# A decoder layer on one core: the memory's keys computed with tokens on the partitions, and turned over DRAM

## The chip, the cores and the metric

The kernel runs on one core of a Trainium2 chip. The metric is the device time of one execution in microseconds (us). The kernel before takes 364.72 us, the median of 3 runs (364.56 to 364.76). The engines are named as in the profile: PE multiplies matrices, DVE, ACT and POOL work elementwise, SP issues most of the transfers. Each engine works through its own instructions in order and waits for the others by semaphores.

## The reference, cut to what matters

One decoder layer on 256 tokens of width 1024: a causal pooling mixer beside a self-attention, an output projection and a LayerNorm; then an attention with four heads into 256 memory tokens; then a gated feed-forward. All is float32. The change is in the keys of the memory attention:

```python
mix = jnp.concatenate([pool_out, attn_out], axis=-1) @ w_out[l]
h = layer_norm(DEEPNORM_ALPHA * h + mix, ln1_g[l], ln1_b[l])
# memory attention
q = (h @ w_xq).reshape(B_, S_, XATTN_HEADS, XATTN_HEAD_DIM)
kv = mem @ w_xkv
k = kv[..., :D].reshape(B_, M, XATTN_HEADS, XATTN_HEAD_DIM)
v = kv[..., D:].reshape(B_, M, XATTN_HEADS, XATTN_HEAD_DIM)
s = jnp.einsum('bshd,bmhd->bhsm', q, k) * (XATTN_HEAD_DIM ** -0.5)
```

`mem @ w_xkv[:, :1024]` gives 256 x 1024 keys. The scores contract over the head's width, so the keys must stand with that width on the partitions.

## The kernel before

Every product is made of three: each operand is split into a high part (`h`, a cast by ACT to float32r) and a low part (`l`, what is left, by DVE), and high x high, high x low and low x high are added in PSUM. A weight goes through three steps: SP loads it into a raw tile (`w27r`, one of 7 buffers), ACT casts it (`w27h`), DVE subtracts (`w27l`); high and low tiles have 9 buffers each. The class `Stream` orders this: `tick`, called by a projection as it goes, prepares the next weight every `pace`-th time, and not while `held` is true. A raw buffer that a split has freed is loaded at once with the weight 7 places further on (`fetch`, L111 to L124), and that load stands in SP's queue at this place of the program.

PE's order of work is the program's. The stages that matter here: values and scores of the self-attention, `u` (L730), the memory's keys `xk` (L742), in whose midst `mix_pool` (L712) puts eight matmuls; the output projection `mix` (L912) with `attend` (L682) in its midst; the memory's values `xv` (L944); the queries `xq` (L968), one head at a time, between them the scores `xscores` (L974).

The keys are made by `proj_s`: a 128 x 128 block of the weight is stationary and the memory's 256 tokens move past it, high and low side by side (512 columns), and then the weight's low part with the high tokens alone (256 columns). The result has the width on the partitions, as the scores want it. ACT and DVE add the two halves out of PSUM into a tile (L748, L749); `xk_split` makes `xkTh` and `xkTl` of it in the course of the mix.

The values are made by `proj_rows`, the other way round: 128 tokens are stationary, and a row block of the weight, 128 x 1024, moves past in pieces of 512 columns. The result has the tokens on the partitions.

Three other tiles are turned between the two forms by way of DRAM (`turned`, `landed`, L494 to L512): DVE transposes 32 x 32 blocks, one transfer writes the tile to DRAM, four read it back by quarters of 32 partitions. The self-attention's probabilities `p` do this on SP's queue (tiles `ps`, `pd`, then `pt0` and `pt1`), and so does the first LayerNorm's result (`hs`, `hd`, `hr`), which becomes `h1Th` and `h1Tl`, the operand of the queries. The memory attention's probabilities (`xs`, `xd`, `xr`) use POOL's queue.

A transfer waits until the one eight places ahead of it in its queue has landed, since they share a semaphore.

Of the kernel before, what the change touches and what calls it, by code (L numbers as in the profile page):

```python
# [8 lines left out]
F32 = mybir.dt.float32  # L9
F32R = mybir.dt.float32r  # L10
# [23 lines left out]
PR_BUFS = 6  # L34
# [5 lines left out]
def r32(t):  # L40
    return t.bitcast(F32)


class Stream:
# [121 lines left out]
    def next(self):  # L166

        i = len(self.tiles)
        return i + (2 if i < len(self.items) and self.items[i][0] == "sums" else 1)
# [28 lines left out]
    def rows(self, numbers):  # L198

        return sum(self.count(i) for i in numbers)  # L200
# [8 lines left out]
@with_exitstack  # L209
def decoder_layer(  # L210
    ctx: ExitStack, tc: tile.TileContext, x, x_t, mem_t, w_qkv, w_u, w_pool, pool_scale, w_out,
    ln1_g, ln1_b, w_xq, w_xk, w_xkv, w_xo, ln2_g, ln2_b, w_gu, w_down, ln3_g, ln3_b, out,
):
    nc = tc.nc
    cp = ctx.enter_context(tc.tile_pool(name="const", bufs=1))
    wp = ctx.enter_context(tc.tile_pool(name="weights", bufs=W_BUFS))
    ap = ctx.enter_context(tc.tile_pool(name="acts", bufs=A8_BUFS))
    sp = ctx.enter_context(tc.tile_pool(name="small", bufs=3))
# [7 lines left out]
    def a8(name, dt=F32):  # L226
        return ap.tile([P, KD, S], dt, tag="a8", name=name)
# [8 lines left out]
    ws = Stream(nc, wp)  # L236

    def cols(w, c):

        return ws.add(w[c])  # L240

    def rows(w, k0, c0, nk=1, width=D):
        return ws.add(w[k0 * P:(k0 + nk) * P, c0:c0 + width].rearrange("(k p) n -> p k n", p=P), 1)
# [15 lines left out]
    ws.cuts[0] = [slice(0, 128), slice(128, 256), slice(256, 512)]  # L259
    ws.steps = {0: (ws.cuts[0], halves), 1: (halves, [slice(0, 512)])}  # L260
    c_u = [cols(w_u, c) for c in range(2)]
    c_xk = [cols(w_xk, c) for c in range(4)]
    c_mix = [rows(w_out, k, 0) for k in range(KD)]
    c_xv = [rows(w_xkv, k, D) for k in range(KD)]
    c_xq = [cols(w_xq, c) for c in range(4)]
# [15 lines left out]
    for c in range(NFC):  # L281
        c_gu.append(ws.add(w_gu[c], 4))
        n = c - LAG
# [17 lines left out]
    def sides(name):  # L301
        return [ap.tile([P, KD // 2, 2, S], F32R, tag="a8", name=f"{name}{i}") for i in range(2)]
# [4 lines left out]
    xT, mT = sides("xT"), sides("mT")  # L307
# [33 lines left out]
    def load_norm(tag, i, v):  # L341
# [16 lines left out]
        out=tri[:, P:], in_=tri[:, P:], compare_op=OP.is_ge, fill=NEG, base=0,  # L358
# [22 lines left out]
    ALL = slice(None)  # L381
# [242 lines left out]
    def scores():  # L624
        wide = {}
        for hq in range(2):
            for j in range(2):
                wide[hq, j] = bank(f"ps{hq}{j}").rearrange("p (h s) -> p h s", h=2)
        for t in range(T):
            w = (t + 1) * P  # L630
            for hq in range(2):
                for h in range(2):
                    for j in range(2):
                        hs = slice(j * HD, (j + 1) * HD)
                        hp = 2 * hq + h
# [29 lines left out]
    def probs_out(hp):  # L665
        blocks = []
        for j in range(2):
            for t in range(T):
                pr = probs[hp // 2, t, j][:, hp % 2]
                blocks.append((3 * j + t, pr.rearrange("p (m c) -> p m c", c=P)))  # L670
        turns[hp] = turned(blocks, 6, "p")
# [24 lines left out]
    sums = {}  # L696
# [26 lines left out]
    def do_v():  # L723
        pieces = [(t, 0, 512) for t in range(T)]
        acc = {piece: accbank("pv") for piece in pieces}
        yield from proj_rows(acc, c_v, lambda k: token(xT, k), pieces, True, True, True)
        for piece in pieces:
            nc.scalar.copy(vt[:, piece[0], :], acc[piece])

    def do_u():  # L730
        for c in range(2):
            pss = [halved((accbank if c else bank)(f"pu{f}")) for f in range(2)]
            yield from proj_s(pss, c_u[c], xT)
            for f, ps in enumerate(pss):
                dst = upad[:, 2 * c + f, PADW:]
                nc.scalar.copy(dst, ps[:, 1])
                nc.vector.tensor_add(dst, ps[:, 0], dst)  # L737
                windows(2 * c + f)

    xkT = (a8("xkTh", F32R), a8("xkTl", F32R))  # L740

    def do_xk():  # L742
        for c in range(4):
            pss = [halved((accbank if c < 3 else bank)(f"pxk{f}")) for f in range(2)]
            yield from proj_s(pss, c_xk[c], mT)
            sums = xk_sums[c] = sp.tile([P, 2, S], F32, name="pr", bufs=PR_BUFS)
            for f, ps in enumerate(pss):
                nc.scalar.copy(sums[:, f], ps[:, 1])  # L748
                nc.vector.tensor_add(sums[:, f], ps[:, 0], sums[:, f])  # L749

    xk_sums = {}

    def xk_split(c):
        split(*[half[:, 2 * c:2 * c + 2, :] for half in xkT], xk_sums[c])

    v, u, xk = do_v(), do_u(), do_xk()
    ws.pace = 3
    def quads(name):
# [5 lines left out]
    pss = scores()  # L764
# [13 lines left out]
    run(u)  # L778
    ws.held = False
    ws.pace = 1  # L780
    run(xk, 6)
    ws.held = True
    run(xk, 11)
    ws.held = False
    pool_diff(0)
    pool_diff(1)
    probs_in(0)
    probs_in(1)
    run(xk, 2)
    probs_out(2)  # L790
    probs_out(3)
    run(xk, 2)
    pool_diff(2)
    run(xk, 2)
    pool_diff(3)
    ws.pace = 3
    run(xk, 9)
    probs_in(2)
    probs_in(3)
    ws.pace = 2  # L800
    run(xk, 6)
    ws.held = True
    run(xk, 12)
    mix_pool()
    ws.held = False
    run(xk, 5)
    ws.held = True
    run(xk)
    ws.held = False
# [7 lines left out]
    class Norm:  # L817
# [11 lines left out]
        def sum(self, c0, c1, acc):  # L829
            s = slice(c0, c1)  # L830
            nc.vector.scalar_tensor_tensor(self.r[:, s], self.tok[:, s], ALPHA, acc, op0=OP.mult, op1=OP.add)
# [74 lines left out]
    def h1_split(t):  # L906
        raw = turns1[t].rearrange("p i k b -> p k i b")
        for k0 in (0, 4):
            h, l = [h[:, k0:k0 + 4, t * P:(t + 1) * P].rearrange("p k (i b) -> p k i b", i=4) for h in h1T]
            split(h, l, raw[:, k0:k0 + 4])  # L910

    mix = project(c_mix, lambda k: (cT[0][:, k], cT[1][:, k]), 4)  # L912
    run(mix, 2)
    xk_split(0)
    xk_split(1)
    ws.held = True
    run(mix, 2)
    load_norm("g", 1, ln1_g)()
# [1 line left out]
    run(mix, 1)  # L920
    attend()
    ws.held = False
    run(mix, 2)
    xk_split(2)
    xk_split(3)
    norms = [Norm(1, xt[:, t, :], h1[:, t, :]) for t in range(T)]
    for half in HALVES:
        norms[0].add(*half, until(mix)[1])
# [9 lines left out]
    run(mix)  # L938
    ws.held = False
    h1T = (a8("h1Th", F32R), a8("h1Tl", F32R))  # L940

    xv = [ap.tile([P, T, D], F32R, tag="a8", name=f"xv{i}") for i in range(2)]

    def do_xv():  # L944
        acc = {piece: (bank if piece == PIECES[2] else accbank)("xv") for piece in PIECES}
# [4 lines left out]
    def xv_split(t):  # L950

        for _, c0, c1 in PIECES[2 * t:2 * t + 2]:
            split(xv[0][:, t, c0:c1], xv[1][:, t, c0:c1], xvs[t, c0, c1])

    xvs = {}
    gv = do_xv()
    run(gv, 6)
    h1_split(0)
    run(gv, 4)
    h1_split(1)  # L960
    run(gv)
    xv_split(0)


# [203 lines left out]
    acc = {}  # L1168
# [8 lines left out]
    for c in range(1, NFC):  # L1177
        sgs.append(sp.tile([P, 2, T, P], F32, name="sg", tag="pr", bufs=PR_BUFS))
        pss = {t: second[t] if c == 1 else accbank("pg") for t in range(T)}
# [185 lines left out]
    for c0, c1, left in quarters:  # L1365
# [2 lines left out]
        store(1, norm.r, c0, c1)  # L1368


_INS = ["x", "x_t", "mem_t", "w_qkv", "w_u", "w_pool", "pool_scale", "w_out", "ln1_g", "ln1_b", "w_xq", "w_xk",
        "w_xkv", "w_xo", "ln2_g", "ln2_b", "w_gu", "w_down", "ln3_g", "ln3_b"]


# [41 lines left out]
```

## Time and profile before

| | |
|---|---|
| median of 3 runs | 364.72 us |
| the profiled execution's own time | 364.02 us |
| its span, first to last instruction | 362.2 us |
| PE busy | 356.8 us, 98% |
| DVE busy | 313.1 us, 86% |
| ACT busy | 201.9 us, 56% |
| POOL busy | 61.0 us, 17% |
| moved by DMA | 89.22 MB, 246 GB/s on average |

The profile is of one execution. 1.8 us of its time lie outside the span. A matmul's end is modelled and overlaps the next one's start, so the pace of a stage is read from where its first matmul and the next stage's first matmul stand in the chain of waits, not from the durations.

### The profile page before, as it was taken

The numbers are of one execution on the slowest core, as the hardware profiler recorded it, in microseconds if no ns is written. First come the engines' busy times: TensorE is split into PE (matmuls) and PEld (weight loads), VectorE is DVE, ScalarE is ACT, GpSimd is POOL, SyncE is SP. The second block draws the span as 40 slices with busy tenths as digits, with TensorE's granted clock in tenths as the row PEclk, the third lists the DMA queues.
The fourth block names the chain that finished last, engine by engine and source line by source line (L and its number), as shares of the span: only waits on it lengthen the run. The fifth ranks groups of instructions, "written<-read, shape, count | busy, mean of one in ns | idle before, by whom it ended". The sixth has DMA issues, their size and how long they took to land.

```text
span 362.2 us, 5435 instructions
## 1 busy us (share of the span) xinstructions
PE 356.8 (98%) x1843; PEld 304.4 (84%) x1843; DVE 313.1 (86%) x477; ACT 201.9 (56%) x317; POOL 61.0 (17%) x82
## 2 busy tenths in 40 slices
PE   8999999999999999999999999999999999999995
PEld 7887888888888899988888888888888888888884
DVE  5878999985999888775879989999998999879984
ACT  5857776375362765465037636744754754679301
POOL 1000009400000003320110024225303413400000
PEclk9999999999999999999999999999999999999999
DMA  7997388799936996943107887888879779658211
GB/s 247 419 419 281 116 286 314 227 329 316 371 148 208 375 373 219 340 137 135 58 0 239 320 283 243 292 293 302 297 253 346 246 256 313 218 172 260 85 58 58
DMA packets 35771, 89.22 MB, mean 246 GB/s; under 512 B 4256, under 2 KB 14368, under 8 KB 35616
## 3 DMA queue, kind: packets, MB, share of 16 engines
q1 hardware_dynamic: 34544, 86.92, 68.5%
q0 software_dynamic: 624, 1.57, 1.3%
q10 hardware_dynamic: 576, 0.39, 0.3%
q8 instruction: 14, 0.23, 0.2%
q14 instruction: 13, 0.11, 0.1%
HBM read 81.53 MB, written 7.34 MB: 245 GB/s over the span
## 4 chain that ended last, share of the span: by engine, by line
PE 98%; DMA 1%; ACT 0%; ACTq 0%; issue 0%
PE pg L376 11%; PE pg L375 11%; PE pg L374 11%; PE pxq L392 6%; PE pqk L548 6%; PE acc L374 6%; PE acc L376 6%; PE acc L375 6%; PE pxk L418 4%; PE x L376 2%; PE x L375 2%; PE x L374 2%; PE pxk L414 2%; PE pu L418 2%; PE xv L376 2%; PE xv L375 2%
## 5 line engine op out<-in xcount | busy, mean ns | idle before, releaser
L1098 POOL TENSOR_TENSOR sraw<-gr 128x128 f32<-128x128 f32 x9 | 8.7, 962 | 94.8 <-DMA gr<-gd 69.7
L847 POOL TENSOR_TENSOR rs<-mv,mhalf 128x1 f32<-128x1 f32 x6 | 4.4, 731 | 104.3 <-DVE mv L845 104.3
L703 POOL TENSOR_TENSOR win<-upad 128x271 f32<-128x271 f32 x4 | 3.5, 882 | 52.5 <-DVE upad L737 52.5
L478 ACT CAST h2Th<-tp 128x512 fp32r<-128x512 f32 x4 | 2.4, 588 | 14.5 <-PE tp L489 14.5
L1099 POOL TENSOR_TENSOR sraw<-sraw,gr 128x128 f32<-128x128 f32 x9 | 10.2, 1134 | 0.7
L1078 ACT ACTIVATE sg<-pg 128x256 f32<-128x256 f32 x22 | 7.8, 379 | 2.8 <-PE pg L376 2.7
L479 DVE TENSOR_TENSOR gTl<-gr,gTh 128x512 fp32r<-128x512 f32 x11 | 8.6, 780 | 0.7 <-ACT gTh L478 0.7
L478 ACT CAST gTh<-gr 128x512 fp32r<-128x512 f32 x11 | 6.8, 614 | 3.7 <-DMA gr<-gd 3.7
L1100 POOL TENSOR_TENSOR sraw<-gr 128x128 f32<-128x128 f32 x9 | 8.5, 945 | 0.0
L1079 DVE TENSOR_TENSOR sg<-sg,pg 128x256 f32<-128x256 f32 x22 | 8.3, 413 | 0.1
L510 POOL DMA_DIRECT2D xr<-xd x12 | 6.6, 554 | 8.7 <-DMA xd<-xs 6.3
L607 ACT ACTIVATE pr<-pr,mx 128x256 f32<-128x256 f32 (+1 forms) x12 | 5.5, 460 | 4.5 <-DVE mx L653 4.5
L607 ACT ACTIVATE xpr<-xs,mx 128x256 f32<-128x256 f32 x8 | 3.7, 470 | 7.6 <-DVE mx L618 7.6
L499 DVE STREAM_TRANSPOSE gs<-sg 128x512 f32<-128x512 f32 x11 | 7.7, 701 | 0.1
L478 ACT CAST S<-sraw 128x384 fp32r<-128x384 f32 (+1 forms) x9 | 4.7, 523 | 5.0 <-POOL sraw L1100 5.0
L502 POOL DMA_DIRECT2D xd<-xs x3 | 1.9, 629 | 33.4 <-DVE xs L499 33.4
L1336 ACT ACTIVATE minus<-ident 128x128 f32<-128x128 f32 x1 | 0.3, 311 | 12.8 <-DVE r L858 12.8
L852 DVE SCALAR_TENSOR_TENSOR r<-r,mv,g 128x512 f32<-128x512 f32 (+1 forms) x10 | 7.0, 727 | 0.2
L838 DVE BATCH_NORM_STATS2 st<-r 128x6 f32<-128x512 f32 (+1 forms) x10 | 6.4, 637 | 0.3
L1103 POOL TENSOR_TENSOR S<-gr,sraw 128x128 f32<-128x128 f32 x8 | 6.6, 828 | 0.0
L748 ACT COPY pr<-pxk 128x256 f32<-128x256 f32 x8 | 2.6, 376 | 7.2 <-PE pxk L414 7.2
L981 PE MATMUL xs<-xkTh,xq 128*128 128x256 f32 x32 | 6.4, 283 | 0.0
(1363 smaller groups left out, 1409.2 us busy)
## 6 DMA issues: line engine op xcount, KB each, us to landing
gd<-gs SPq DMA_DIRECT2D x11, 256.0 KB, 5.6
gr<-gd SPq DMA_DIRECT2D x44, 64.0 KB, 2.0
pd<-ps SPq DMA_DIRECT2D x4, 384.0 KB, 4.1
pt<-pd SPq DMA_DIRECT2D x16, 96.0 KB, 5.7
g<-in_ln_g SPq DMA_DIRECT2D x3, 512.0 KB, 5.4
b<-in_ln_b SPq DMA_DIRECT2D x3, 512.0 KB, 7.2
wr<-in_w_qkv SPq DMA_DIRECT2D x5, 256.0 KB, 4.6
mr<-in_mem_t SPq DMA_DIRECT2D x1, 1024.0 KB, 11.8
```

The source lines that it names most:

```text
L374: nc.tensor.matmul(ps, wa, ya, start=start, stop=False, skip_group_check=part)
L375: nc.tensor.matmul(ps, wa, yb, start=False, stop=False, skip_group_check=part)
L376: nc.tensor.matmul(ps, wb, ya, start=False, stop=stop, skip_group_check=part)
L392: nc.tensor.matmul(pss[f], w[:, s], y, start=k == 0 and f == 0 and n == 0, stop=k == KD - 1 and n == 2, skip_group_check=True)
L418: nc.tensor.matmul(pss[f], hi[:, s], both, start=k == 0, stop=False, skip_group_check=True)
L478: nc.scalar.copy(h, ps)
L479: nc.vector.tensor_sub(l, ps, r32(h))
L548: nc.tensor.matmul(qk[i][f][:, n], w[:, c * P:(c + 1) * P], both[:, n], start=k == 0 and n.start == 0 and (n.stop == 2 or part in first), ...
L607: nc.scalar.activation(dst[:, j, :], src[:, j, :], AF.Exp, bias=mx[:, j:j + 1], scale=sign, accum_out=sm[:, j:j + 1])
L1098: nc.gpsimd.tensor_add(s1, a21, a22)
L1099: nc.gpsimd.tensor_sub(s2, s1, a11)
L1100: nc.gpsimd.tensor_sub(s3, a11, a21)
```

## The change

The keys are made like the values: `do_xk` keeps 128 memory tokens stationary and moves row blocks of `w_xkv[:, :1024]` past them, into four banks of PSUM that it holds to its end, two of them (`accbank`) among the four that the mix accumulates in. Then DVE transposes the four banks into two tiles `ms`, and POOL writes them to DRAM (`md`, 512 KB each). After `attend` POOL reads them back in eight transfers into a tile of their own, `xkr`. `xk_split` comes near the end of the values, two splits of 128 x 1024. The copy of the weight by columns, `w_xk`, is gone. The calls of `run(xk, n)` are scaled, as a step is now three matmuls of 512 columns.

```diff
-    c_xk = [cols(w_xk, c) for c in range(4)]
+    c_xk = [rows(w_xkv, k, 0) for k in range(KD)]
...
     def do_xk():
-        for c in range(4):
-            pss = [halved((accbank if c < 3 else bank)(f"pxk{f}")) for f in range(2)]
-            yield from proj_s(pss, c_xk[c], mT)
-            sums = xk_sums[c] = sp.tile([P, 2, S], F32, name="pr", bufs=PR_BUFS)
-            for f, ps in enumerate(pss):
-                nc.scalar.copy(sums[:, f], ps[:, 1])
-                nc.vector.tensor_add(sums[:, f], ps[:, 0], sums[:, f])
...
-    def xk_split(c):
-        split(*[half[:, 2 * c:2 * c + 2, :] for half in xkT], xk_sums[c])
+        pieces = [(t, c0, c0 + 512) for t in range(T) for c0 in (0, 512)]
+        acc = {piece: (bank if piece[0] else accbank)("pxk") for piece in pieces}
+        for k in range(KD):
+            for t, c0, c1 in pieces:
+                hi, lo = ws.get(c_xk[k], 0)
+                three(acc[t, c0, c1], pair(token(mT, k), ALL, slice(t * P, (t + 1) * P)),
+                      (hi[:, c0:c1], lo[:, c0:c1]), k == 0, k == KD - 1)
+                if t and c0:
+                    ws.done(c_xk[k], 0)
+                yield
+        for t in range(T):
+            turnk[t] = turned([(4 * n, acc[piece].rearrange("p (m c) -> p m c", c=P))
+                               for n, piece in enumerate(pieces[2 * t:2 * t + 2])], KD, "m", nc.gpsimd)
+
+    def xk_in(t):
+        if not t:
+            xk_rows[0] = ap.tile([P, T, 4, KD, 32], F32, tag="a8", name="xkr")
+        turnk[t] = landed(turnk[t], KD, "m", nc.gpsimd, raw=xk_rows[0][:, t])
+
+    def xk_split(t):
+        split(*[x[:, :, t * P:(t + 1) * P].rearrange("p m (i b) -> p m i b", i=4) for x in xkT],
+              turnk[t].rearrange("p i m b -> p m i b"))
...
     run(mix, 2)
-    xk_split(0)
-    xk_split(1)
...
     attend()
     ws.held = False
+    for t in range(T):
+        xk_in(t)
     run(mix, 2)
-    xk_split(2)
-    xk_split(3)
...
     h1_split(1)
+    xkT = (a8("xkTh", F32R), a8("xkTl", F32R))
+    run(gv, 2)
+    xk_split(0)
+    run(gv, 2)
+    xk_split(1)
     run(gv)
```

SP's queue in the last third of `xk`, where the second half of the probabilities (`pt1`, printed as `pt`) is read back for `attend`. `w35r` to `w37r` are loads of raw weights:

```order
 L123 DMA w34r<-in_w_out 128x1024
 L123 DMA w35r<-in_w_xkv 128x1024
-L510 DMA pt_861<-pd 32x4x192 x8
 L123 DMA w36r<-in_w_xkv 128x1024
+L510 DMA pt_844<-pd 32x4x192 x8
 L123 DMA w37r<-in_w_xkv 128x1024
```

The load of `w36` now stands ahead of the eight reads instead of behind them, and the eighth read now waits for `w36r` to land, where it waited for `w35r`.

DVE's order from the last split of the LayerNorm's result (`h1Tl`) to the split of the first head's queries (`xq`), in the values and the first queries:

```order
 L479 TENSOR_TENSOR h1Tl<-hr,h1Th 128x4x128 x2
 L149 TENSOR_TENSOR w48l<-w48r,w48h 128x1024
+L479 TENSOR_TENSOR xkTl<-xkr,xkTh 128x8x128
 L149 TENSOR_TENSOR w49l<-w49r,w49h 128x1024
+L479 TENSOR_TENSOR xkTl<-xkr,xkTh 128x8x128
 L149 TENSOR_TENSOR w50l<-w50r,w50h 128x1024
-L479 TENSOR_TENSOR xv_1223<-xv,xv_1222 128x512 x2
+L479 TENSOR_TENSOR xv_1356<-xv,xv_1355 128x512 x2
 L149 TENSOR_TENSOR w51l<-w51r,w51h 128x1024
 L149 TENSOR_TENSOR w52l<-w52r,w52h 128x1024
-L483 SCALAR_TENSOR_TENSOR xq_1466<-pxq,xq_1465 128x512
+L483 SCALAR_TENSOR_TENSOR xq_1425<-pxq,xq_1424 128x512
```

The two splits of the keys, 1024 elements wide each, now stand between the LayerNorm's result and the queries' split.

DVE's order at the end of `xk` and in the mix:

```order
 L149 TENSOR_TENSOR w31l<-w31r,w31h 128x1024
-L749 TENSOR_TENSOR pr<-pxk_920,pr 128x256
-L749 TENSOR_TENSOR pr<-pxk_921,pr 128x256
+L499 STREAM_TRANSPOSE ms<-pxk 128x4x4x32 x4
 L149 TENSOR_TENSOR w32l<-w32r,w32h 128x1024
 L149 TENSOR_TENSOR w33l<-w33r,w33h 128x1024
-L479 TENSOR_TENSOR xkTl<-pr,xkTh 128x512 x2
```

Four transposes of 128 x 512 out of PSUM take the place of two additions, and two splits of 128 x 512 are gone; two more are gone behind `w35l`.

## Rows read from the trace of the kernel before

**Rows 1.** The page, part 4: the chain that ended last, shares by engine

```profile
PE 98%; DMA 1%; ACT 0%; ACTq 0%; issue 0%
```

**Rows 2.** Chain of waits, 52 to 77 us: start, us, engine, tile, line, count

```profile
52.61 3.65 PE pxk L418 x16
56.26 1.91 PE pxk L414 x16
...
70.00 1.73 PE pm L716 x8
...
76.61 0.23 PE acc L374
```

**Rows 3.** Chain of waits, 100 to 132 us

```profile
101.43 0.23 PE xv L374
...
123.19 7.55 PE pxq L392 x63
130.74 1.32 PE xs L981 x11
```

**Rows 4.** The tile pxk: nanoseconds min/median/max, first and last start

```profile
L748 ACT COPY pr<-pxk x8: 372/377/380, 58.1 to 76.8; 128x256 f32<-128x256 f32 x8
L749 DVE TENSOR_TENSOR pr<-pxk,pr x8: 406/410/418, 59.7 to 78.3; 128x256 f32<-128x256 f32 x8
```

**Rows 5.** The page, part 5: busy us, mean ns | idle before, releaser

```profile
L499 DVE STREAM_TRANSPOSE gs<-sg 128x512 f32<-128x512 f32 x11 | 7.7, 701 | 0.1
...
L502 POOL DMA_DIRECT2D xd<-xs x3 | 1.9, 629 | 33.4 <-DVE xs L499 33.4
```

**Rows 6.** Timeline of DVE: start, us, instruction, [idle before it <- releaser]

```profile
75.64 1.23 DVE L149 TENSOR_TENSOR w30l<-w30r,w30h 128x1024 fp32r<-128x1024 f32 x1 [0.46 <-ACT w30h L147]
...
90.13 1.28 DVE L479 TENSOR_TENSOR xkTl<-pr,xkTh 128x512 fp32r<-128x512 f32 x2
...
121.34 1.29 DVE L479 TENSOR_TENSOR h1Tl<-hr,h1Th 128x512 fp32r<-128x512 f32 x2
...
124.47 1.23 DVE L149 TENSOR_TENSOR w49l<-w49r,w49h 128x1024 fp32r<-128x1024 f32 x1 [0.70 <-ACT w49h L147]
...
130.28 0.68 DVE L483 SCALAR_TENSOR_TENSOR xq<-pxq,xq 128x512 fp32r<-128x512 f32 x1
```

**Rows 7.** Timeline of SP's queue

```profile
72.61 0.46 SPq L123 DMA_DIRECT2D w35r<-in_w_xkv  x1
74.62 5.90 SPq L510 DMA_DIRECT2D pt<-pd  x8
80.62 0.38 SPq L123 DMA_DIRECT2D w36r<-in_w_xkv  x1
...
114.46 0.38 SPq L123 DMA_DIRECT2D w47r<-in_w_xq  x1
```

**Rows 8.** DMA issues, 45 to 130 us: KB each, median us to landing

```profile
hd<-hs SPq DMA_DIRECT2D x2, 512.0 KB, 2.6
...
w35r<-in_w_xkv SPq DMA_DIRECT2D x1, 512.0 KB, 7.6
...
w47r<-in_w_xq SPq DMA_DIRECT2D x1, 512.0 KB, 4.6
```

**Rows 9.** The tile pt: all its transfers, then only the one issued last

```profile
DMA to landing us min/median/max: 2.0/5.7/8.4
...
DMA to landing us min/median/max: 3.5/3.5/3.5
```

**Rows 10.** Timeline of PE in attend

```profile
85.37 0.65 PE L690 MATMUL po<-pt,vt 128*64 128x256 f32 x4
```

**Rows 11.** Stretches: us, busy PE, PEld, DVE, ACT, POOL, PEclk, DMA share, GB/s

```profile
80.00:82.00 2.00, 2.00 (x11) 1.65 (x10) 2.00 (x3) 0.12 (x1) 0.00 (x0) 1.00 0.69 170
...
92.00:94.00 2.00, 2.00 (x10) 1.67 (x9) 2.00 (x3) 1.61 (x2) 0.00 (x0) 1.00 1.02 418
...
102.00:104.00 2.00, 2.00 (x11) 1.65 (x10) 2.00 (x3) 1.38 (x2) 0.00 (x0) 1.00 0.00 0
```

More of the change, by code (lines that the diff above doesn't have):

```diff
@@ L211, in decoder_layer @@
     ctx: ExitStack, tc: tile.TileContext, x, x_t, mem_t, w_qkv, w_u, w_pool, pool_scale, w_out,
-    ln1_g, ln1_b, w_xq, w_xk, w_xkv, w_xo, ln2_g, ln2_b, w_gu, w_down, ln3_g, ln3_b, out,
+    ln1_g, ln1_b, w_xq, w_xkv, w_xo, ln2_g, ln2_b, w_gu, w_down, ln3_g, ln3_b, out,
 ):
@@ L738, in do_u @@
                 windows(2 * c + f)
-    xkT = (a8("xkTh", F32R), a8("xkTl", F32R))
+    turnk = {}
     def do_xk():
-        for c in range(4):
-            pss = [halved((accbank if c < 3 else bank)(f"pxk{f}")) for f in range(2)]
-            yield from proj_s(pss, c_xk[c], mT)
-            sums = xk_sums[c] = sp.tile([P, 2, S], F32, name="pr", bufs=PR_BUFS)
-            for f, ps in enumerate(pss):
-                nc.scalar.copy(sums[:, f], ps[:, 1])
-                nc.vector.tensor_add(sums[:, f], ps[:, 0], sums[:, f])
-    xk_sums = {}
-    def xk_split(c):
-        split(*[half[:, 2 * c:2 * c + 2, :] for half in xkT], xk_sums[c])
+        pieces = [(t, c0, c0 + 512) for t in range(T) for c0 in (0, 512)]
[11 more added lines that the diff above has]
+                               for n, piece in enumerate(pieces[2 * t:2 * t + 2])], KD, "m", nc.gpsimd)
+    xk_rows = {}
+    def xk_in(t):
[5 more added lines that the diff above has]
+              turnk[t].rearrange("p i m b -> p m i b"))
     v, u, xk = do_v(), do_u(), do_xk()
@@ L780, in decoder_layer @@
     ws.pace = 1
-    run(xk, 6)
+    run(xk, 3)
     ws.held = True
-    run(xk, 11)
+    run(xk, 5)
     ws.held = False
@@ L788, in decoder_layer @@
     probs_in(1)
-    run(xk, 2)
+    run(xk, 1)
     probs_out(2)
     probs_out(3)
-    run(xk, 2)
+    run(xk, 1)
     pool_diff(2)
-    run(xk, 2)
+    run(xk, 1)
     pool_diff(3)
     ws.pace = 3
-    run(xk, 9)
+    run(xk, 5)
     probs_in(2)
@@ L800, in decoder_layer @@
     ws.pace = 2
+    run(xk, 3)
+    ws.held = True
     run(xk, 6)
-    ws.held = True
-    run(xk, 12)
     mix_pool()
     ws.held = False
-    run(xk, 5)
+    run(xk, 2)
     ws.held = True
@@ L940, in decoder_layer @@
     h1T = (a8("h1Th", F32R), a8("h1Tl", F32R))
-    xv = [ap.tile([P, T, D], F32R, tag="a8", name=f"xv{i}") for i in range(2)]
     def do_xv():
@@ L960, in decoder_layer @@
     h1_split(1)
+    xkT = (a8("xkTh", F32R), a8("xkTl", F32R))
[3 more added lines that the diff above has]
+    xk_split(1)
     run(gv)
+    xv = [ap.tile([P, T, D], F32R, tag="a8", name=f"xv{i}") for i in range(2)]
     xv_split(0)
@@ L1368, in decoder_layer @@
         store(1, norm.r, c0, c1)
-_INS = ["x", "x_t", "mem_t", "w_qkv", "w_u", "w_pool", "pool_scale", "w_out", "ln1_g", "ln1_b", "w_xq", "w_xk",
-        "w_xkv", "w_xo", "ln2_g", "ln2_b", "w_gu", "w_down", "ln3_g", "ln3_b"]
+_INS = ["x", "x_t", "mem_t", "w_qkv", "w_u", "w_pool", "pool_scale", "w_out", "ln1_g", "ln1_b", "w_xq", "w_xkv", "w_xo", "ln2_g", "ln2_b", "w_gu", "w_down", "ln3_g", "ln3_b"]
 def kernel(**inputs):
@@ L1403 @@
     given["w_qkv"] = np.concatenate([first.ravel(), w_in[3 * P:, 512:1536].ravel(), blocks(w_in[:, 1536:], pairs)])
-    given["w_u"], given["w_xk"] = chunks(given["w_in"][:, :512]), chunks(given["w_xkv"][:, :D])
+    given["w_u"] = chunks(given["w_in"][:, :512])
     given["w_xq"] = chunks(given["w_xq"])
```

## The prediction

> **What bounds the kernel now.** I read the chain that ended last first. Its shares by engine [rows 1] leave 98% to PE: the kernel is as long as PE's work, and a saving on another engine is worth nothing by itself. Then the same chain in order of time around the change. The keys begin at 52.61 and the mix at 76.61, with 1.73 of `pm` (the pooling mixer's matmuls) inside [rows 2]; the values run from 101.43 to 123.19, then the queries and the first scores [rows 3]. No wait stands between them. So the gain is what PE saves in the keys, and each rival is a wait that PE doesn't have today. For those I read the timelines of SP and DVE up to the instruction that would release PE, and last the DMA share by stretch, since the change adds traffic.
>
> **The keys on PE.** Before they cost 76.61 - 52.61 - 1.73 = 22.27 us: four chunks of 16 matmuls of 512 columns and 16 of 256, 3.65 and 1.91 a chunk [rows 2], which is 228 and 119 ns each. Removed are 128 matmuls, added 96 of 512 columns. The columns stay 49,152. What is added needs no estimate: the values are the same loop over the same stationary tokens with a weight of the same size, 8 row blocks x 4 pieces x 3 = 96 matmuls, in 123.19 - 101.43 = 21.76 us, 227 ns each [rows 3]. The gain is 22.27 - 21.76 = 0.51, and this is all that the change can give on PE.
>
> The Trainium skill ("TensorE: Matmul & The Clock Gate", section Back-to-back issue gap) gives N/2.4 + 2.5 ns for an isolated gap at the full clock, 216 and 109 ns. By it the keys would go from 64 x 325 ns = 20.8 us to 96 x 216 ns = 20.7 us, an estimate of 0.1 saved. The rows are above it, and by more at 256 columns, so the 0.51 of the rows stands.
>
> **DVE and ACT around the keys.** ACT loses eight copies of 377 ns, DVE eight additions of 410 ns [rows 4] and four splits of 0.64 (a row of two takes 1.28 [rows 6]). DVE gains four transposes, 0.70 each from SBUF [rows 5]; no row shows one from PSUM, so between 0.7 and twice that, taken at 0.75. All of it lies beside PE. It could reach PE in one place: the mix's third and fourth bank are the keys' first two, and PE wants them 6 and 9 matmuls after its start, 1.36 and 2.04 us. In DVE's order one weight split stands before the transposes. The one that stands in its place now began at 75.64, after waiting for ACT, and took 1.23 [rows 6]; PE and the pooling mixer come about 0.4 earlier, so the two transposes run from about 76.5 to 78.0, and PE, at the mix from 76.1, wants the banks at 77.5 and 78.1. Cost nothing, cover 0.1 to 0.3; from PSUM at twice the price it costs up to 1.4.
>
> **The reads for `attend`.** In SP's queue `w36r` moves ahead of the eight reads of `pt1`. The last read now goes out when `w36r` has landed. Before, it went out when `w35r` had, 72.61 + 7.6 = 80.2 [rows 7, 8], and landed 3.5 later, at 83.7 [rows 9]. A load of 524 KB at the 418 GB/s of a full stretch [rows 11] takes 1.25, so the last read goes out at 81.45 and lands at 84.95. PE wants it at the last group of `attend`, 85.37 before [rows 10] and 84.86 now: a wait of 0.1. With the quickest landing, 2.0 [rows 9], it is early by 1.4. The hop adds to it: DVE's transposes end near 78.0 and 79.5, and POOL then writes twice 524 KB, 1.25 each, against the same reads. DMA is idle for 0.62 in 80 to 82 [rows 11]. Of the first write 0.63 doesn't fit there, and about half of this lies ahead of the last read: 0.3. If both writes go ahead, the wait is 0.1 + 2.5 = 2.6. I take 0.4, with ends at 0 and 2.6, near the low one because the measured landing gives 0.1.
>
> **The key splits at the end of the values.** DVE has from the end of the LayerNorm's split, 121.34 + 1.29 = 122.63, to the queries' split, 130.28 to 130.96 [rows 6]. PE wants that at the ninth matmul of the first scores: 130.74 + 8 x 0.12 = 131.70 [rows 3]. Two splits are put between, 1.14 each by the spacing of weight splits, and take up the 0.70 that DVE waited there [rows 6]: 1.58 later, at 132.54, counted from the same start. PE comes at 131.70 - 0.51 + 0.4 = 131.59. Alone it would cost 0.95. The cover is an earlier start: DVE loses 1.28 at 90.13 [rows 6], and what follows there, the first LayerNorm and its hop, is a row of DVE work that moves up by that much; so does the load of `w47`, which goes out behind the hop at 114.46 and lands 4.6 later [rows 7, 8], just ahead of the split in question. With 1.2 earlier and the 0.4 of `attend` later, DVE is done at 131.7, the same 0.1 as PE. I take 0; the ends are 0 and, if the start is half a us later than today, 1.4.
>
> The 10 transfers that POOL issues, about 0.6 each [rows 5], cost nothing: POOL has no other work until the LayerNorm.
>
> **The sum.** -0.51 + 0.4 + 0 = -0.1. On the profiled execution's own 364.02 (its span, 362.2, and 1.8 around it) that is 363.9; the median is 0.7 above that execution, so I carry the difference to it: 364.72 - 0.1 = 364.6.
>
> **Rivals.** *All waits are hidden.* Then the 0.51 stays: 364.2. For it: the last read can land 1.4 early, and the hop's writes may use what is idle. Against it: three covers of 0.1 to 0.3 would have to hold at once.
>
> *The hop's traffic makes the key splits late.* Place: DVE between the LayerNorm's split and the queries' split. The hop moves 2.1 MB, 5.0 us at 418 GB/s, in a stretch where DMA is full but for 0.62 in 80 to 82 and all of 102 to 104 [rows 11]; some 2 us are left over, just where the LayerNorm's hop (2.6 to land [rows 8]) and `w47` are to come early. Then the start is not 1.2 earlier but up to 0.5 later, and PE waits 0.95 to 1.4 at the first scores beside the 0.4 in `attend`: -0.51 + 0.4 + 1.3 = +1.2, 365.9. It decides from the point where `w47r` goes out later than about 113.5. Against it: it takes all 5.0 us as additive, though SP's small reads leave a third of 80 to 82 unused. The Trainium skill ("DMA: Bandwidth & Descriptors", section Issuing engines are not separate DMA queues) says that transfers started by SP and by POOL run on the same 16 engines and interleave, and that a second issuing engine saves only the time to issue; by that rule the hop takes its full 5.0 from SP's loads, and this rival would be the forecast.
>
> *The transposes or the reads hold PE in the mix.* By the ends above 1.4 or 2.6 in place of 0 and 0.4: 366.0 to 366.8. For it: the cover at the banks is 0.1 to 0.3. Against it: both ends take the worst of each row.
>
> **How the numbers follow.** About 0.2%, 0.73 us, is what a measurement of this kernel can tell from no change. The forecast has a chance of 0.36, all waits hidden 0.28, the late key splits 0.28, the hold in the mix 0.08. The forecast's own range is 364.2 to 365.2. Faster than 363.99 needs more than the 0.51 that PE can save: 0.05, out of the second case. Slower than 365.45 hold the last two cases but for 0.03, and a little of the forecast's upper end: 0.35. The rest, 0.60, is within. The range goes from 364.0, under the hidden case, to 366.1, which leaves about 0.1 above.
>
> **What would show it.** In the changed profile 96 matmuls of `pxk` should take 21.7 to 21.8 without `pm`; another pace makes the first term wrong. In `attend` a wait of PE for `pt` of 0.1 to 1.0 should stand before the last groups; none means the hidden case. At the first scores a wait of PE for DVE's `xq` of 0.9 or more, with `w47r` issued after 113.5, shows the late splits. A wait of `acc` for DVE's transposes at the mix's third bank shows the last rival. The forecast is wrong if PE saves 0.5 and the time moves by more than 0.7 either way.

## The result, and the profile after

The changed kernel takes 368.13 us, the median of 4 runs (367.33 to 368.46), beside 364.73 us for the kernel before in the same runs (364.56 to 364.76). The ratio is 1.0091, 95% interval 1.0074 to 1.0109: slower by 3.4 us, outside the range of 364.0 to 366.1. The profiled execution took 368.03, with a span of 366.3 where the kernel before had 362.2. In the table of the experiments the medians are of all runs, while the ratios leave out four runs that took over 1.5% more than the fastest of their kernel (two of writes only, one each of late reads and held loads).

The page, part 4, shares by engine of the chain that ended last, answers to [rows 1]:

```profile
PE 64%; DVE 13%; DMA 13%; issue 4%; ACT 3%; SPq 2%; POOL 1%; DVEq 0%; ACTq 0%; POOLq 0%
```

PE is still 98% busy, but 26% of the chain now runs over DVE and DMA, and 36% over everything but PE: work ahead of PE has become what sets the end. What PE waited for (us in total, times, longest):

```profile
PE xs L995 <- DVE xq L483: 1.2, 1, 1.2
...
PE pxq L392 <- DVE h1Tl L479: 0.6, 1, 0.6
PE xo L375 <- DVE xst L479: 0.3, 1, 0.3
PE xs L995 <- ACT xq L482: 0.3, 1, 0.3
```

None of the four was there before. `xs` are the scores of the memory attention; `xo` multiplies its probabilities with the values, and `xst` is the split of these probabilities behind their own hop. PE's timeline, where the stages begin (answers to [rows 2, 3, 10]):

```profile
53.03 0.40 PE L374 MATMUL pxk<-w19h,mT 128*128 128x512 f32 x1
...
76.55 0.39 PE L374 MATMUL acc<-w27h,cTh 128*128 128x512 f32 x1
...
85.59 0.65 PE L690 MATMUL po<-pt,vt 128*64 128x256 f32 x4
...
124.14 0.39 PE L392 MATMUL pxq<-h1Tl,w43h 128*128 128x256 f32 x1 [0.62 <-DVE h1Tl L479]
...
132.08 0.39 PE L995 MATMUL xs<-xkTh,xq 128*128 128x256 f32 x1 [0.25 <-ACT xq L482]
...
134.49 0.74 PE L995 MATMUL xs<-xkTh,xq 128*128 128x256 f32 x4 [1.19 <-DVE xq L483]
```

Counted against the same matmul of the kernel before, PE is 0.6 late when the keys begin (the first stage, whose program is the same in both, went slower in this execution; in the second profile of the kernel before it is 0.4 late too), 0.1 late at the mix, 0.2 at the values, 1.0 after the wait for `h1Tl`, 3.0 after the two waits for the queries' split, 3.8 after the wait for `xst`, and 4.1 at the end. Each wait costs 0.2 to 0.5 more than its idle time.

SP's queue, answers to [rows 7]:

```profile
72.30 0.39 SPq L123 DMA_DIRECT2D w36r<-in_w_xkv  x1
73.86 6.34 SPq L510 DMA_DIRECT2D pt<-pd  x8
...
102.86 0.33 SPq L502 DMA_DIRECT2D hd<-hs  x1
108.20 1.75 SPq L510 DMA_DIRECT2D hr<-hd  x4
110.05 0.38 SPq L502 DMA_DIRECT2D hd<-hs  x1
113.48 2.93 SPq L510 DMA_DIRECT2D hr<-hd  x4
116.51 0.38 SPq L123 DMA_DIRECT2D w47r<-in_w_xq  x1
```

The LayerNorm's first write (`hd`) goes out 0.76 earlier than before and takes 5.3 to land in place of 2.6; its second stands behind the late reads and takes 3.4; `w47r` goes out 2.05 later. The stretches show why (the columns of [rows 11]: PEclk, DMA share and GB/s at the end):

```profile
80.00:82.00 2.00, 2.00 (x11) 1.63 (x10) 1.88 (x2) 0.00 (x0) 0.49 (x1) 1.00 1.09 340
92.00:94.00 2.00, 2.00 (x10) 1.66 (x9) 2.00 (x3) 0.78 (x1) 0.00 (x0) 1.00 1.03 289
102.00:104.00 2.00, 2.00 (x11) 1.65 (x10) 1.97 (x4) 1.74 (x2) 0.00 (x0) 1.00 1.03 420
```

The idle time of 80 to 82 and of 102 to 104 is gone, and in 92 to 94 full engines move 289 GB/s in place of 418, while the hop is read back. The kernel before had more idle time there than [rows 11] show. Its stretches from 80 to 106, the same columns:

```profile
80.00:90.00 10.00, 10.00 (x65) 8.05 (x64) 5.67 (x7) 4.42 (x8) 0.00 (x0) 1.00 0.91 287
90.00:98.00 8.00, 8.00 (x37) 6.63 (x36) 7.93 (x11) 3.61 (x4) 0.00 (x0) 1.00 1.07 404
98.00:102.00 4.00, 4.00 (x20) 3.30 (x19) 3.90 (x8) 2.53 (x3) 0.56 (x1) 1.00 0.74 260
102.00:106.00 4.00, 4.00 (x19) 3.33 (x18) 3.86 (x8) 2.43 (x3) 0.00 (x0) 1.00 0.32 131
```

By these shares 4.1 of the 26 us were idle; in the changed kernel the same four stretches have 1.02 to 1.04. DVE's timeline, answers to [rows 5, 6]:

```profile
77.13 2.50 DVE L499 STREAM_TRANSPOSE ms<-pxk 128x512 f32<-128x512 f32 x4
...
94.89 0.68 DVE L843 SCALAR_TENSOR_TENSOR r<-xt,acc 128x512 f32<-128x512 f32 x1
...
122.26 1.22 DVE L149 TENSOR_TENSOR w47l<-w47r,w47h 128x1024 fp32r<-128x1024 f32 x1 [3.90 <-ACT w47h L147]
123.40 1.28 DVE L479 TENSOR_TENSOR h1Tl<-hr,h1Th 128x512 fp32r<-128x512 f32 x2
...
128.01 1.22 DVE L479 TENSOR_TENSOR xkTl<-xkr,xkTh 128x1024 fp32r<-128x1024 f32 x1
...
133.75 0.68 DVE L483 SCALAR_TENSOR_TENSOR xq<-pxq,xq 128x512 fp32r<-128x512 f32 x1
```

DVE reaches the LayerNorm 1.0 earlier (94.89 against 95.88 before). It loses 0.2 of this to the load of the LayerNorm's bias `b`, a third transfer that lands late: 16.2 us after its issue, 9.7 in the kernel before. The chain of waits has it:

```profile
83.32 16.22 DMA b<-in_ln_b
```

Then DVE stands idle for 3.9 us until `w47` is there. `h1Tl` is 2.06 late, the queries' split 3.47.

### The profile page after: what moved, and what is told of

Its sections match the earlier page's. It is cut to its first block, busy times and chain, and to the rows that moved or that the text cites. A ratio compares the mean times of both kernels' runs of the same rounds, so it can differ in the third digit from the quotient of the medians.

```text
span 366.3 us, 5373 instructions
## 1 busy us (share of the span) xinstructions
PE 358.9 (98%) x1811; PEld 304.1 (83%) x1811; DVE 313.3 (86%) x471; ACT 199.4 (54%) x307; POOL 68.7 (19%) x92
## 4 chain that ended last, share of the span: by engine, by line
PE 64%; DVE 13%; DMA 13%; issue 4%; ACT 3%; SPq 2%; POOL 1%; DVEq 0%; ACTq 0%; POOLq 0%
PE pg L375 11%; PE pg L374 11%; PE pg L376 11%; DMA b<-in_ln_b 4%; PE pqk L548 4%; PE acc L374 3%; PE acc L375 3%; PE acc L376 3%; PE pxq L392 3%; PE x L375 2%; PE x L374 2%; DMA w49r<-in_w_xq 2%; PE x L376 2%; DMA xr<-xd 2%; DMA wr<-in_w_qkv 2%
## 5 line engine op out<-in xcount | busy, mean ns | idle before, releaser
L1112 POOL TENSOR_TENSOR sraw<-gr 128x128 f32<-128x128 f32 x9 | 9.5, 1060 | 92.9 <-DMA gr<-gd 50.3
L1114 POOL TENSOR_TENSOR sraw<-gr 128x128 f32<-128x128 f32 x9 | 9.5, 1055 | 0.0
L995 PEld LDWEIGHTS xs<-xkTh,xq 128*128 128x128 f32 x32 | 5.2, 191 | 1.9 <-DVE xq L483 1.4
L703 POOL TENSOR_TENSOR win<-win 128x269 f32<-128x269 f32 (+2 forms) x6 | 6.7, 1109 | 0.5
```

Source lines behind the costliest of these rows:

```text
L703: nc.gpsimd.tensor_add(nxt[:, 2 * n - 1:], cur[:, 2 * n - 1:], cur[:, n - 1:PADW + S - n])
L995: nc.tensor.matmul(ps[:, t, :], w, xkT[n][:, 2 * h + kk], start=not (low or t or kk or n), stop=bool(low and kk), skip_group_check=True)
L1112: nc.gpsimd.tensor_add(s1, a21, a22)
L1114: nc.gpsimd.tensor_sub(s3, a11, a21)
```

## The experiments

Theory A: the hop adds DMA work where the engines are full, the LayerNorm's hop and `w47` land late, and PE waits for whichever transfer is then last. Rival B: the two splits in DVE's order are the loss. Theory C and rival D came with the second series. C: the reads of `pt` stand on an edge, and the hop's writes push them over it in some executions. D: the traffic costs the same wherever it is put. Each series shares its runs of the kernel before. The changed kernel itself differs by 1.7 us between its two series, for a reason that no run shows, so versions of different series can't be told apart more finely than that. "Profiled" is the time of the one execution that left the profile, often one of the slower; "waits" are PE's largest behind the first stage in that profile, in us (`r` is the LayerNorm's first addition, `po` the products of `attend`, `tp` a transpose on PE); "w31" is the landing time of the load of `w31` in that profile, which goes out near 60, ahead of everything the change adds.

| kernel | median, range (runs) | before | ratio, 95% interval | profiled | waits | w31 |
|---|---|---|---|---|---|---|
| changed | 368.13, 367.33 to 368.46 (4) | 364.73 | 1.0091, 1.0074 to 1.0109 | 368.03 | `h1Tl` 0.6, `xq` 1.5 | 7.3 |
| changed again | 369.80, 369.22 to 371.50 (5) | 364.73 | 1.0149, 1.0129 to 1.0170 | 369.33 | `pt` 2.5 | 9.2 |
| no hop | 365.20, 364.05 to 366.13 (12) | 364.52 | 1.0019, 1.0009 to 1.0028 | 365.90 | `xst` 1.1 | 8.0 |
| early splits | 368.26, 366.58 to 371.05 (6) | 364.52 | 1.0095, 1.0078 to 1.0112 | 371.05 | `pt` 3.9 | 10.1 |
| no hop, early splits | 364.67, 363.94 to 365.76 (11) | 364.52 | 1.0004, 0.9994 to 1.0014 | 364.67 | `xst` 0.3 | 7.2 |
| traffic alone | 367.79, 367.36 to 368.91 (5) | 364.52 | 1.0097, 1.0083 to 1.0112 | 367.52 | `h1Tl` 1.0 | 8.5 |
| writes only | 367.80, 365.01 to 372.85 (8) | 364.73 | 1.0062, 1.0031 to 1.0092 | 369.42 | `pt` 2.2 | 9.7 |
| pt first, early splits | 368.32, 367.08 to 371.39 (6) | 364.73 | 1.0119, 1.0085 to 1.0153 | 371.39 | `r` 2.1, `pt` 0.9 | 9.7 |
| late reads | 369.37, 367.27 to 373.21 (6) | 364.73 | 1.0127, 1.0094 to 1.0160 | 373.21 | `pt` 3.2, `h1T` 1.4 | 9.3 |
| spread | 369.86, 367.89 to 371.85 (6) | 364.57 | 1.0147, 1.0123 to 1.0172 | 369.80 | `h1T` 3.1 | 7.9 |
| late writes | 373.63, 370.20 to 373.96 (6) | 364.57 | 1.0231, 1.0204 to 1.0258 | 373.43 | `h1T` 5.1, `r` 0.9 | 9.6 |
| held loads | 369.00, 366.30 to 372.10 (7) | 364.57 | 1.0096, 1.0064 to 1.0128 | 369.06 | `pt` 2.5, `h1Tl` 1.0 | 9.7 |
| turn on PE | 370.64, 369.19 to 371.08 (4) | 364.57 | 1.0159, 1.0143 to 1.0174 | 370.60 | `tp` 3.5 | 8.8 |
| turn in the gap | 366.35, 366.25 to 367.33 (5) | 364.43 | 1.0055, 1.0043 to 1.0067 | 366.30 | `po` 0.8 | 9.5 |
| half traffic | 367.34, 366.87 to 368.40 (5) | 364.43 | 1.0084, 1.0070 to 1.0098 | 367.34 | `r` 1.3, `h1Tl` 0.6 | 7.2 |
| order alone | 364.48, 364.14 to 366.11 (12) | 364.43 | 1.0007, 0.9996 to 1.0018 | 364.14 | none | 9.2 |
| before again | 364.46, 364.24 to 366.97 (11) | 364.43 | 1.0006, 0.9994 to 1.0019 | 364.46 | none | 8.1 |

### Traffic or splits: two by two, and the traffic by itself

**No hop.** 

> The changed kernel without the hop: DVE's four transposes go straight into the tile xkr, nothing is written to DRAM and nothing read back (so the keys' blocks are not exchanged between the quarters of partitions; this exchange is what is left out, 2.1 MB of traffic). The two splits stay where the change put them. Theory A (the hop's traffic keeps the DMA engines full to 106, so the LayerNorm's hop and the load of w47 come 2.06 late, and the two splits add 1.58 to that): w47r goes out at 113.2 to 114.0 in place of 116.51, no wait of PE at the first queries, 0 to 0.3 at the first scores, 364.2 to 365.0 us; 0.6 more if the first stage is as late as in the changed kernel's profile. Rival B (it is the two splits in DVE's order alone): the wait at the first scores stays at 1.0 or more, 367.0 to 368.0 us.

```diff
-            turnk[t] = turned([...], KD, "m", nc.gpsimd)
+            xk_in(t)                     # only takes the tile xkr
+            for n, piece in enumerate(pieces[2 * t:2 * t + 2]):
+                nc.vector.transpose(turnk[t][...], acc[piece]...)
```

**Early splits.** 

> The changed kernel with its hop, but the two key splits stand ahead of the LayerNorm's splits, after the second and fourth step of the values. Theory A: the traffic is the same, so w47r still goes out near 116.5 and PE still waits 0.6 at the first queries; the queries' split comes 2 earlier and the wait of 1.2 at the first scores goes: 366.2 to 366.8 us. Rival B: all of the loss goes, 364.2 to 364.8 us.

```diff
 gv = do_xv()
+    run(gv, 2); xk_split(0); run(gv, 2); xk_split(1); run(gv, 2)
-    run(gv, 6)
     h1_split(0)
...
-    run(gv, 2); xk_split(0); run(gv, 2); xk_split(1)
```

**Both.** 

> Both edits at once: no hop (the exchange of blocks between quarters of partitions is left out) and the key splits ahead of the LayerNorm's. Theory A: no wait of PE is left and the 0.51 us that the keys save on PE stays: 364.0 to 364.6 us, the same as no hop alone within 0.4. Rival B: the same as early splits alone. If a loss of 0.6 in the first stage belongs to the changed program and not to one execution, all of these stand 0.6 higher.

**Traffic alone**, in the kernel before. 

> The kernel before with the traffic alone: after the keys POOL writes 1 MB to DRAM (four writes of 256 KB out of the last tile of the keys) and after attend reads 1 MB back by eight transfers into a tile that nobody uses. Nothing else is changed. Theory A: the LayerNorm's hop lands 2 us later, w47r goes out near 116.5, PE waits 0.6 to 1.0 at the first queries and not at the first scores, 365.3 to 365.9 us. Rival B: the traffic costs nothing, 364.6 to 364.9 us.

```diff
+        for t in range(T):               # at the end of do_xk
+            turnk[t] = hp.tile([P, 4, KD * 32], F32, name="md")
+            for n in range(2):
+                nc.gpsimd.dma_start(turnk[t][:, 2 * n:2 * n + 2], xk_sums[3])
...
     attend()
     ws.held = False
+    for t in range(T):
+        xk_in(t)
```

Without the hop 365.20: 2.7 of the 3.4 us are gone, with the splits where the change put them (A's range ends at 365.0, or 365.6 with a late first stage; the wait of 1.1 for `xst` was not in it). SP's queue then runs as it should:

```profile
102.38 0.33 SPq L502 DMA_DIRECT2D hd<-hs  x1
104.97 1.75 SPq L510 DMA_DIRECT2D hr<-hd  x4
...
113.22 0.38 SPq L123 DMA_DIRECT2D w47r<-in_w_xq  x1
```

`hd` lands in 2.6 and `w47r` goes out at 113.22, the 1.2 earlier that the prediction's cover asked for. The splits are worth 0.5 (365.20 to 364.67), with intervals that overlap. With the hop, moving them gains nothing (368.26), so B falls; A's 366.2 to 366.8 was missed as well. The traffic alone costs the kernel before 3.3 us, nearly the loss of the change, with neither rows nor splits; A named the place (`w47r` at 117.13, a wait of 1.0 for `h1Tl`) but priced it at a third: PE is 1.7 late at the first queries and 3.4 behind `xo`, where it waits again, as it also does without the hop. The early splits brought what no theory had: a wait of 3.9 for `pt`, in the slowest of the six executions.

The hop's DMA work is read from the page, part 3 (queue, kind, packets, MB, share of 16 engines). POOL's queue before, and after:

```profile
q0 software_dynamic: 624, 1.57, 1.3%
```

```profile
q0 software_dynamic: 1296, 3.67, 3.0%
```

3.0% of 366.3 less 1.3% of 362.2 is 6.3 us for 2.1 MB; the prediction had 5.0. This counts POOL's packets alone, not what SP's loads lose beside them.

### Where the wait stands, and what decides it

**Changed again.** 

> The changed kernel once more, nothing edited, for its spread and a second profile. In the kernel with early splits PE waited 3.9 us for the reads of pt in attend, and then ran 6 us at half the clock; in the first profile of the changed kernel it did not wait there at all, though both have the same program up to that place. Theory C (the reads of pt stand on an edge, and the hop's writes push them over it in some executions): PE waits for pt again here, or the times spread by 2 us or more. Theory A: the wait is 0 to 0.3, and the loss is again at the first queries and scores; 367.3 to 368.5 us by both.

In this execution PE waited for nothing at the queries. It lost its time in `attend`. The chain of waits, 74 to 92 us:

```profile
74.51 9.07 DMA w36r<-in_w_xkv
83.58 0.02 issue
83.60 4.77 DMA pt<-pd
88.37 0.14 issue
88.51 0.66 PE po L690 x4
```

The last read of `pt` goes out when `w36r` has landed, 9.07 after its issue, and takes 4.77 beside the hop's writes: the mechanism of "Reads for attend", at its far end. PE idled 2.51, and then the clock fell (stretches, columns as above):

```profile
86.00:90.00 4.00, 1.49 (x11) 1.20 (x12) 0.69 (x1) 0.58 (x2) 2.83 (x6) 0.99 1.01 362
90.00:94.00 4.00, 4.00 (x13) 3.11 (x12) 3.71 (x4) 4.00 (x6) 1.57 (x3) 0.58 1.02 318
94.00:98.00 4.00, 4.00 (x19) 3.34 (x18) 3.88 (x4) 1.80 (x2) 0.00 (x0) 1.00 1.03 284
```

After the idle time the granted clock is 0.58 in 90 to 94, mostly the lower of its two levels: 13 matmuls where the full clock does 19. PE is 3.1 late at the last `po` and 4.7 to 5.0 at the first scores. C holds as a second place of the same loss: this series has a wait for `pt`, and a median 1.7 above the first, which lies outside the 367.3 to 368.5 of both theories.

**Writes only.** 

> The changed kernel with the hop's two writes of 512 KB but without the eight reads: DVE's transposes go into xkr, POOL writes xkr to DRAM, and the splits take xkr as it is (the exchange of blocks between the quarters of partitions is left out). Theory A: half of the traffic, in a stretch that had 0.62 us of idle DMA; DMA is done by 103.5 in place of 106, the LayerNorm's first write lands in 2.6 to 4 in place of 5.3, 365.2 to 366.4 us. Theory C: the writes alone are what pushes the reads of pt, PE waits there in some executions, 366 to 368 us.

```diff
     # as without the hop, and behind the two transposes:
+            via = hp.tile([P, 4, KD * 32], F32, name="md")
+            nc.gpsimd.dma_start(via, turnk[t].rearrange("p j m b -> p j (m b)"))
```

PE waits 2.2 for `pt`, as C has it; the times run from 365.01, the level without the hop, to 372.85. Its q0 has 2.0% of 367.6, so the writes are 2.6 us of DMA work and the reads the other 3.6.

**Order alone**, in the kernel before. 

> The kernel before with one edit: the second half of the probabilities is read back three steps later, so that the load of w36 goes out ahead of the reads of pt in SP's queue, as in the change. No hop, the keys by columns. Theory A: the reads of pt have cover enough without the hop's writes: 364.4 to 365.2 us, no wait for pt. If the order in SP's queue alone makes pt late: 366 us or more, with a wait for pt of 1 us or more.

```diff
-    probs_in(2); probs_in(3)
     ws.pace = 2
-    run(xk, 6)
+    run(xk, 3); probs_in(2); probs_in(3); run(xk, 3)
```

**Before again.** 

> The kernel before once more, for a second profile. The first reads of pt took 8.53 us to go out in its first profile and 7.2 to 10 in the changed versions, ahead of any traffic of the hop. If that is a spread of the landings that every kernel has, its second profile may show 7 to 10 too, and its time stays 364.2 to 365.2 us, since the cover ahead of attend takes it up.

The order alone costs nothing measurable, in a profile whose `w31` took 9.2 to land; three of its twelve executions took 365.6 to 366.1, and one of the eleven of "before again" 366.97. So the table sorts by two things. The second, the landing of `w31`, was only observed, in one profile of each kernel; no run set it. With the hop's full writes out before `attend`, all six profiles whose `w31` landed in 9.2 to 10.1 wait for `pt`, and the two at 7.3 and 8.5 do not. Without those writes, four at 8.8 to 9.6 do not (in one of them, the turn in the gap, PE also comes 2.2 later). The landing isn't fixed in the kernel before either (8.6 and 8.1 in its two profiles, 9.2 in the order alone, the same program up to there); the cover ahead of `attend` takes this up, until the writes use that cover.

### Can the debt be placed where it costs nothing?

**Reads of pt first, early splits.** 

> The changed kernel with the key splits ahead of the LayerNorm's, and with the reads of pt back in front of the load of w36 in SP's queue, as the kernel before has them. Theory C: without the wait for pt only the wait of 0.6 at the first queries is left: 366.0 to 366.8 us, 1.5 or more below early splits alone. Theory A alone (no part of the loss in attend): the same as early splits alone, 367.8 to 368.6 us.

```diff
     ws.pace = 3
-    run(xk, 5)
-    probs_in(2); probs_in(3)
+    run(xk, 3)
+    probs_in(2); probs_in(3)
+    run(xk, 2)
```

The wait for `pt` is 0.9, but DVE now waits 2.0 for `w39`, the LayerNorm's first addition is late, and PE waits 2.1 for its bank (`r`). The gain that C promised is not there; 368.32 lies in the range that A alone gave.

**Late reads.** 

> A version meant to be best: the changed kernel with the reads of pt in front of w36, the hop's eight reads issued after the second half of the LayerNorm (about 106.6 in place of 84.65, where the kernel before leaves the DMA engines half idle), one key split behind the LayerNorm's first split and one behind its second. Theory A: the LayerNorm's first write lands in 2.6 again, w47r goes out at 113.5 to 115, PE waits 0 to 0.6 in all: 364.2 to 365.4 us. Rival D (the traffic costs the same wherever it is put, since the engines only owe it to a later load): 367 us or more.

```diff
     norms[1].finish()
+    for t in range(T):
+        xk_in(t)
     h1_in(0)
```

The hop's reads, issued at 110.19, meet the LayerNorm's second write, which takes 5.6 to land; `w47r` goes out at 121.49, in the slowest of the six executions, where PE waits 3.2 for `pt` too. D's time is right here.

**Spread, late writes, held loads.** 

> The changed kernel with four moves: the reads of pt back in front of w36, the hop's two writes issued by ACT behind attend (about 87 in place of 78.7), the loads of w45 and w46 held back until the LayerNorm's first write has been issued (a millionth number limit in the loader, nothing else), the key splits ahead of the LayerNorm's. Theory A (the hop's 6.3 us of DMA work must be paid where the engines are full, and PE waits for whichever transfer is then last): PE waits for pt 0 as before, the LayerNorm's first write lands in 2.6 to 3.5, w47r goes out at 113 to 115: 364.2 to 365.6 us. Rival D (the debt comes back elsewhere whatever is moved): 367 us or more, with a wait for a weight or for the LayerNorm's hop.

> The changed kernel with the hop's two writes alone moved behind attend (ACT issues them). Theory C (the writes push the reads of pt over the edge in most executions): no wait for pt in any execution, the spread shrinks, and the debt falls on the LayerNorm's hop and the key splits alone: 367 to 368.3 us. If the reads of pt are late by themselves (w36 ahead of them), PE still waits for pt by 1 us or more, 368.5 us or more.

> As the version that spreads the debt, but with the hop's writes where the change has them (about 78.7): reads of pt in front of w36, w45 and w46 held back, key splits early. Theory C: PE waits for pt by 0.5 to 3 us in the profile, and the time is 1 to 3 us above the version with late writes. Theory A without C: both within 0.5.

```diff
     # late writes: the transposes alone in do_xk, and
     attend()
+    for t in range(T):
+        xk_out(t)        # nc.scalar.dma_start(via, turnk[t]...)
...
     # held loads: fetch() stops at w44, and
     h1_out(0)
+    ws.cap = 10 ** 6
+    ws.fetch(ws.freed + RAW_BUFS, nc.sync)
```

Late writes are the worst of all, 373.63, though the wait for `pt` is gone as C said. What PE waited for, and SP's and POOL's queues:

```profile
PE pxq L392 <- ACT h1Th L478: 4.3, 1, 4.3
```

```profile
105.80 0.33 SPq L502 DMA_DIRECT2D hd<-hs  x1
114.41 2.92 SPq L510 DMA_DIRECT2D hr<-hd  x4
```

```profile
97.04 2.39 POOL L510 DMA_DIRECT2D xkr<-md  x4 [28.16 <-DMA md<-ms]
...
101.98 0.59 POOL L866 TENSOR_TENSOR rs<-mv,mhalf 128x1 f32<-128x1 f32 x1
```

The writes land 10 us after ACT issued them, the reads go out at 97, the LayerNorm's own `rs` stands behind them on POOL, and `hd` takes 8.6 to land. Held loads waits for `pt` as C said, but is no slower than the spread. None of the three came to the time that A or C gave it; each moved the wait to another place, and none took the loss away. That no placement exists is not shown.

### Less traffic

**Half traffic.** 

> The hop without DRAM: the blocks go from ms to xkr in 32 transfers of 32 KB within SBUF, POOL issues them from 78.7 on, so 1 MB is moved in place of 2.1 and nothing waits for a first landing; reads of pt in front of w36, key splits early. The same result. Theory A (the loss follows the DMA work): the DMA time of the hop falls from 6.3 to 3 to 4, 365 to 367.5 us, with the waits at the same places and smaller. Rival D (any traffic there costs it all): 368 us or more.

```diff
+            for j in range(4):
+                for i in range(4):
+                    nc.gpsimd.dma_start(turnk[t][32 * j:32 * (j + 1), i], ms[32 * i:32 * (i + 1), j])
```

Queue q0 has 2.2% of 365.6, which leaves 3.3 us of work for the blocks, and the kernel takes 367.34, inside A's range and 0.8 to 2.5 below the changed kernel's two medians. Its interval overlaps those of the changed kernel's first series and of "pt first, early splits", which differs from it only in the hop; that half the work costs less is likely, not shown. Part of what is left is its own: the 32 issues keep POOL until 102.86, and `rs` is 2.4 late.

**Turn on PE, and in the gap.** 

> The keys in rows as in the change, but turned by 16 transposes on PE out of an SBUF copy of the four banks, in the first steps of the values; no hop, no traffic. The same result without the DMA. Theory A: the price is PE's own, 16 transposes at 0.44 us for four, 1.76, less the 0.51 that the rows save: 365.6 to 366.4 us, no wait of PE for pt, for the LayerNorm's split or for the queries'. If the loss of the change came from the keys in rows and not from the hop: 367 us or more.

> The keys in rows, turned on PE, but the 16 transposes stand just ahead of attend, where DVE and ACT are idle for 3.5 us, in place of the values, where the second eight waited 3.5 us for DVE in the last run. No hop. Theory A: 1.76 for the transposes less 0.51: 365.4 to 366.4 us, no wait of PE above 0.5. If the keys in rows cost something themselves: 367 us or more.

```diff
+        for t, c0, c1 in pieces:         # at the end of do_xk, for the hop
+            (nc.vector.tensor_copy if c0 else nc.scalar.copy)(xk_rows[0][:, t, c0:c1], acc[t, c0, c1])
...
     run(mix, 1)
+    xkT = (a8("xkTh", F32R), a8("xkTl", F32R))
+    for t in range(T):
+        for k0 in (0, 4):
+            transpose_tok(xkT, xk_rows[0][:, t, :], t, k0)
     attend()
```

In the values the second eight transposes waited 3.5 for DVE, busy with the LayerNorm, and the granted clock was 0.58 in the 4 us behind: 370.64, a miss that says only where not to put them. Ahead of `attend` 366.35, 1.9 above the kernel before: 1.76 - 0.51 and a wait of 0.8 of `po` for DVE's `xkTl`. This is the fastest kernel with keys in rows and the whole result; it beats the changed kernel, not the kernel before. No version tried beats that.

## Why the prediction was wrong, step by step

- **The keys on PE: right.** 76.55 - 53.03 - 1.73 = 21.79 us, predicted 21.76. Even without the hop this 0.5 does not show in the time (364.67 against 364.52): in that profile PE is 0.1 early at `xo`, waits 0.3 there for `xst`, and is 0.6 late behind it. The prediction read no row behind the first scores.
- **DVE and ACT around the keys: right.** Four transposes from PSUM take 2.50, 0.62 apart; the mix's third bank held PE for 0.1.
- **The reads for `attend`: the mechanism right, its size one execution's.** It took 0.4 out of 0 to 2.6, because the landings of one trace gave 0.1. They are not fixed: the wait was 0 in the first profile of the change and 2.5 in the second. The lower clock that followed most such waits was in no term.
- **The key splits at the end of the values: this step failed.** It counted the cover, a start 1.2 earlier, from DVE's order. DVE was 1.0 earlier, but what follows is no row of DVE work: it goes through DMA, where the hop's backlog lay, and the start came 2.06 later. To that the step's own 1.58 was added as it says: 2.06 + 1.58 = 3.64, measured 3.47 at the queries' split. In place of the 0 that the step took, PE waited 0.6 at the first queries and 1.5 at the first scores. (The 131.70 at which PE wants the split is a place in the chain, 0.16 behind that matmul in the timeline, while DVE's 132.54 is of the timeline; without the cover the cost would have been 1.1, not 0.95.)
- **The rival of the hop's traffic: right place and the condition that it named** (`w47r` after 113.5: 116.51), with half a us where 2.06 came, 5.0 us of DMA work where 6.3 came, and +1.2 where +3.4 came. Its "some 2 us are left over" came out through two errors that cancel, which is luck: the prediction took the engines for full but for 2.6 us, and between 80 and 106 they had 4.1 idle. It got 0.28 where it should have led. The Trainium skill's rule that the prediction quoted ("DMA: Bandwidth & Descriptors", section Issuing engines are not separate DMA queues) speaks for it, and the traces agree: with both queues at work in 92 to 94 the share stays at 1.03, and both together move 289 GB/s, where SP's loads alone moved 418.
- **The sum** set a gain of 0.51 against terms at their low ends, chosen from the margins of a single execution. The traffic was charged once, in `attend`, for 0.3, while its 6.3 us of DMA work met 4.1 us of idle time between 80 and 106.

## What to carry to other kernels

Where DMA has little idle time (here 4.1 of 26 us), the work of a new transfer beyond it comes back as a delay at something that waits for a later landing, and a cover made of DVE time does not hide it: add up the DMA work and the idle time of the whole stretch, not of three samples, before the order of an engine. Take a margin at a landing from the spread of several executions, since a load ahead of the hop landed 7.3 and 9.2 us after its issue in two profiles of the same program. A wait of PE can cost the clock behind it as well: waits of 1.8 to 4.3 us did so in eight profiles here, and one of 2.5 did not.

## What was not expected of the hardware

- Reading the hop back, in runs of 1 KB, kept the engines at a share of 1.03 and moved 289 GB/s in all, where weights alone move 418: 3.6 us for 1 MB, the writes of the same bytes 2.6. The loads beside it slow down too: by these rows 4 KB take 0.23 us of one engine there (4096 x 16 x 1.03 / 289) against 0.16 (4096 x 16 x 1.02 / 418), and in the trace the packets of both queues do. That the short runs are the reason isn't shown.
- The clock: 0.58 granted in 90 to 94, behind an idle time of PE of 2.5 that ended at 88.51, and likewise 0.50 to 0.66 in the 4 us behind waits of 1.8 to 4.3 in seven other profiles; 1.00 behind a wait of 2.5 in the held loads, and behind 1.2 and less in the changed kernel.
- Transposes of 128 x 512 out of PSUM are no dearer than out of SBUF: 0.62 apart, 0.67 to 0.71 each, as in [rows 5].
